# Eight last pairs of a WKV recurrence: every second numerator accumulates in a buffer of the logarithms, and the last pair is finished in two halves

## The chip, the core and the metric

The kernel runs on one core of a Trainium2 chip. The core has five engines with an instruction queue each: TensorE (PE, matrix products into PSUM), VectorE (DVE), ScalarE (ACT, functions such as exponential and logarithm), GpSimd (POOL) and SyncE (SP, which here only issues DMAs). They run beside each other and wait for each other through semaphores. The metric is the time of one execution on the device in microseconds (us), as the median of several executions.

## What is computed

For each of 16 sequences of 2048 steps and each of 256 channels the reference runs a recurrence with a running maximum `pp`, a weighted sum `aa` of the values and a sum `bb` of the weights:

```python
for t in range(seq_len):
    kk, vv = k[b, t, :], v[b, t, :]
    ww = u + kk
    qq = np.maximum(pp, ww)
    e1 = np.exp(pp - qq)
    e2 = np.exp(ww - qq)
    output[b, t, :] = (e1 * aa + e2 * vv) / (e1 * bb + e2 + 1e-08)
    ww = pp - w + kk
    qq = np.maximum(ww, kk)
    e1 = np.exp(ww - qq)
    e2 = np.exp(kk - qq)
    aa = e1 * aa + e2 * vv
    bb = e1 * bb + e2
    pp = qq
```

`k`, `v` and the output are 16 x 2048 x 256 in float32, 33.55 MB each. What matters for this study is the division: every output is a numerator over a denominator.

## The kernel before

**Tiles and stages.** Time is cut into 16 chunks of 128 steps, and the 16 sequences into four groups of four. One such group in one chunk is a "pair" in the kernel's numbering, `n` = 0 to 63, with `c, j = divmod(n, 4)`; a pair's output is a tile of 128 partitions (steps) by 1024 elements, 512 KB. A pair goes through an input part (load, rounding of `k`, logs of weights by TensorE, exponentials by ScalarE at L205, product with the values by VectorE at L214), and four pairs of a chunk together give the chunk's state (`state_*`, a chain of small steps over ScalarE and VectorE that ends in `turn_back`, L297 on TensorE, and `copy_back`, L301 on VectorE). About ten pairs later comes the output part, of which this study speaks:

- `den` (L320): the denominator. Twelve TensorE matmuls (`apply`, L317), three groups of four, into one of the two tiles `X0` and `X1`. The third group of four needs `cb`, the state of the chunk before it is copied back by L301.
- `log_den` (L323): ScalarE takes the logarithm of that tile into a tile `rd` (L325), and gives the `X` tile back.
- `inverse` (L328): ScalarE takes exp(-x) of `rd` in place (L329). So the inverse of the denominator is exp(-ln).
- `num` (L331): the numerator. Twelve matmuls of the same form (L317) into the tile `num`.
- `mult` (L335): VectorE multiplies `num` by `rd` into the output tile `ot` (L337), and gives `num` and `rd` back.
- `store` and `store_rest` (L350, L343): the output tile goes out in three DMAs. SP issues the first half of its columns (256 KB) and one quarter (128 KB); for the pairs from 52 on, GpSimd issues the other quarter (128 KB).

**PSUM and the buffers.** PSUM holds `X0`, `X1` and `num` with two banks each, and one bank each for `TOT` and `TURN`. So there are two buffers for denominators (which the logs of the input part use too, as long as there is input) and one for numerators. `rd` has two buffers, `ot` eight.

**What sets the order.** All instructions of an engine run in the order in which the program emits them. The kernel makes a list of named steps, each with a wished place, the steps that must be emitted before it, and a buffer that it takes and gives back (`step`, and the loop at the end). The loop emits the step with the smallest place whose forerunners are emitted and whose buffer is free in this bookkeeping: `take="X"` needs one of the two `X` tiles, `"N"` the one `num` tile. A step is named here by its kind and pair: LN.59 is the logarithm of pair 59, and so DEN, INV, NUM, MUL, ST (store by SP) and SQ (the quarter by GpSimd).

After the last input pair (63), the output parts of the pairs 55 to 63 are left. In this tail only these steps run, and the last chunk's state chain, which ends in BK.15 (L301); the pairs 60 to 63 need it. TensorE's order there is DEN.56, NUM.55, DEN.57, NUM.56, DEN.58, NUM.57, the turn back of chunk 15, DEN.59, NUM.58, DEN.60, NUM.59 and so on to DEN.63, NUM.62, NUM.63.

Of the kernel before, what the change touches and what calls it, by code (L numbers as in the profile page):

```python
# [7 lines left out]
F32 = mybir.dt.float32  # L8
# [3 lines left out]
ACT = mybir.ActivationFunctionType  # L12
# [3 lines left out]
def kernel(  # L16
# [9 lines left out]
    K = tc.keep_in_program_order  # L26
    PE, DVE, SC, POOL, SP = nc.tensor, nc.vector, nc.scalar, nc.gpsimd, nc.sync
# [5 lines left out]
    D = 2 * Dm  # L33
    NP = 4 * NST
# [5 lines left out]
    BYSP = 3  # L40
    EARLY = 10
    PLAN = "DDDP"
# [1 line left out]
    RS = 2.0 ** -20  # L44
    CAP = 54.0
    BIG = 1e30
    CF = 11
    BYPOOL = 52
    BYQ = "PSSP"
    BYF = 93  # L50
# [7 lines left out]
         "TAIL": {"DEN": -4.36, "LN": -16.54, "INV": 3.8, "NUM": -0.31, "MUL": 4.39, "ST": 14.35, "step": 2.989, "SQ": 26.08},  # L58
         "Z0": {"L": 1, "S": 3, "DEN": 0, "NUM": 6, "TK": 47, "TU": 17, "R": 12},
         "Z": {"DEN": 0, "L": 1, "NUM": 0, "TK": 4, "S": 0, "TU": 1, "R": 0}}  # L60

    consts = ctx.enter_context(tc.tile_pool(name="consts", bufs=1))
    kpool = ctx.enter_context(tc.tile_pool(name="kpool", bufs=NK))
    kppool = ctx.enter_context(tc.tile_pool(name="kppool", bufs=NKP))
    vpool = ctx.enter_context(tc.tile_pool(name="vpool", bufs=NV))
    vbpool = ctx.enter_context(tc.tile_pool(name="vbpool", bufs=NVB))
    rpool = ctx.enter_context(tc.tile_pool(name="rpool", bufs=NRD))
    opool = ctx.enter_context(tc.tile_pool(name="opool", bufs=NOT))
    small = ctx.enter_context(tc.tile_pool(name="small", bufs=2))
    psx = ctx.enter_context(tc.tile_pool(name="psx", bufs=1, space=bass.MemoryType.PSUM))  # L70
    psn = ctx.enter_context(tc.tile_pool(name="psn", bufs=1, space=bass.MemoryType.PSUM))
# [10 lines left out]
    def matrix(name, dt):  # L82
        return consts.tile([128, 128], dt, tag=name, name=name)
# [4 lines left out]
    def rows_of(x, n):  # L88
        c, p = divmod(n, 4)
        return x[4 * p:4 * p + 4, c * TC:(c + 1) * TC, :].rearrange("n t d -> t n d")  # L90

    KR, VR, VB = {}, {}, {}

    def how(n):
        return "D" if n < BYSP else "C" if n < CF else PLAN[n % len(PLAN)]

    def raw(pool, tag):
        return pool.tile([128, 4, Dm], F32, tag=tag, name=tag)

    def load_k(n):  # L100
        if how(n) != "C":
            KR[n] = raw(vpool, "vr") if n < BYSP else raw(kppool, "kf")
            K((SP if n < BYSP else POOL).dma_start(out=KR[n], in_=rows_of(k, n)))  # L103
        else:
            KR[n] = kpool.tile([128, 4, Dm], F32R, tag="kr", name="kr")
            K(POOL.dma_start(out=KR[n], in_=rows_of(k, n)))

    def load_v(n):
        vr = raw(vpool, "vr")
        K((SP if n < BYSP else POOL).dma_start(out=vr, in_=rows_of(v, n)))  # L110
        VR[n] = vr

    WUf = rpool.tile([128, 2, D], F32, tag="rd", name="WUf")[:, 0, 0:Dm]
    WU = consts.tile([128, Dm], BF16, tag="WU", name="WU")

    def row_wu(x, g):
        K(SC.dma_start(out=WUf[g::32, :], in_=bass.AP(tensor=x.tensor, offset=x.offset, ap=[[0, 4], list(x.ap[0])])))

    K(DVE.memset(WUf, 0.0))
    load_k(0)  # L120
    row_wu(w, 0)
    row_wu(u, 1)
    K(SC.preload_act_table_set("natural_log_exp_and_others"))
    M1, I1 = matrix("M1", F32), matrix("I1", F32)
    K(DVE.memset(M1, -1.0))
# [47 lines left out]
    mats = {name: matrix(name, BF16) for name in ("Id", "IdN", "S", "SN")}  # L173
# [11 lines left out]
    X = [psx.tile([128, 2, D], F32, tag=f"X{a}", name=f"X{a}") for a in range(2)]  # L185
# [119 lines left out]
    RD, NUM, OT = {}, {}, {}  # L305
# [17 lines left out]
    def log_den(n, a):  # L323
        rd = rpool.tile([128, 2, D], F32, tag="rd", name="rd")
        K(SC.activation(rd, X[a], ACT.Ln, scale=RS))  # L325
        RD[n] = rd

    def inverse(n):  # L328
        K(SC.activation(RD[n], RD[n], ACT.Exp, scale=-1.0))  # L329

    def num(n):  # L331
        NUM[n] = psn.tile([128, 2, D], F32, tag="num", name="num")
        apply(NUM[n], n, ("SN", "IdN"), 0)

    def mult(n):  # L335
        o = opool.tile([128, 4, Dm], F32, tag="ot", name="ot")
        K(DVE.tensor_mul(o.rearrange("p (i n) d -> p i (n d)", i=2), NUM.pop(n), RD.pop(n)))  # L337
        OT[n] = o

    def piece(n, h, queue):  # L340
# [17 lines left out]
    ops, free = {}, {"K": NK, "KP": NKP, "V": NV, "N": 1, "RD": NRD, "OT": NOT, "VB": NVB}  # L358

    def step(name, place, fn, args=(), after=(), take=None, give=(), mode=0):  # L360
        ops[name] = dict(place=place, fn=fn, args=args, after=list(after), take=take, give=give, mode=mode)

    for n in range(NP):
        c, j = divmod(n, 4)
        early = n < BYSP
        put = lambda key: n + P[key][j]
        lead = SOON * max(0.0, 1 - n / UNTIL)
        m = n + LAG - lead
        tail = n >= NP - LAG
        place = lambda key: m + (P["TAIL"][key] + (n - NP + LAG) * P["TAIL"]["step"] if tail else P["OUT"][key][j])  # L370
        kb = "V" if early else "KP" if how(n) != "C" else "K"
        if n:
            step(("LK", n), n + P["LK"], load_k, (n,), [("LK", n - 1)], kb)
        else:
            free["V"] -= 1
        step(("LV", n), n + P["LV"], load_v, (n,), [("LV", n - 1)] + ([("LK", n)] if n else []), "V")
        if how(n) != "C":
            step(("RK", n), put("RK"), round_k, (n,), [("LK", n), ("RK", n - 1)], "K", [kb])
        for q in range(2):
            step(("R", q, n), n + P["R"][q], rows, (n, q), ["wu", ("R", 1 - q, n - 1 + q)], "X", mode=3)  # L380
            step(("L", q, n), n + P["L"][q], logs, (n, q), [("R", q, n), ("LK", n), ("RK", n), ("L", 1 - q, n - 1 + q)], None,
                 ["K"] if q else [], 1)
            step(("X", q, n), n + P["X"][q], exps, (n, q), [("L", q, n), ("NUM", n - RING), ("S", n - RING)], None, ["X"])
        step(("CV", n), put("CV"), cast_v, (n,), [("LV", n), ("CV", n - 1)], "VB", ["V"])
        step(("TV", n), put("TV"), times_v, (n,), [("X", 1, n), ("CV", n), ("TV", n - 1)], None, ["VB"])
        step(("S", n), put("S"), sums, (n,), [("TV", n), ("S", n - 1)] + ([("CS", c - 1)] if j == 0 else []), mode=2)
        if j == 3:
            s = P["STATE"][0 if c == 0 else 2 if c == NST - 1 else 1]
            for i, (name, fn, *after) in enumerate((
                    ("CS", copy_sums, ("S", n)), ("TU", turn, ("CS", c), ("CH", c - 1)), ("SL", state_logs, ("TU", c)),  # L390
                    ("FR", state_frames, ("SL", c), ("SN", c - 1)), ("OF", state_offsets, ("FR", c)),
                    ("SW", state_weights, ("OF", c)), ("CH", state_chain, ("SW", c), ("KP", c - 1)),
                    ("SS", state_spread, ("CH", c)), ("TK", turn_back, ("SS", c), "mats"), ("BK", copy_back, ("TK", c)),
                    ("SN", state_next, ("OF", c)), ("KP", state_keep, ("CH", c)))):
                if not (name in ("SN", "KP") and c + 1 == NST):
                    step((name, c), n + s[i] - lead * SHARE, fn, (c,), after, mode=1)
        step(("DEN", n), place("DEN"), den, (n,), [("BK", c), ("DEN", n - 1), "mats"], "X", mode=3)
        step(("LN", n), place("LN"), log_den, (n,), [("DEN", n), ("INV", n - 1)], "RD", ["X"])
        step(("INV", n), place("INV"), inverse, (n,), [("LN", n)])
        step(("NUM", n), place("NUM"), num, (n,), [("BK", c), ("TV", n), ("NUM", n - 1), "mats"], "N", mode=3)  # L400
        step(("MUL", n), place("MUL"), mult, (n,), [("NUM", n), ("INV", n), ("MUL", n - 1)], "OT", ["N", "RD"])
        step(("ST", n), place("ST"), store, (n,), [("MUL", n), ("ST", n - 1)], None, [] if shared(n) else ["OT"])
        if shared(n):
            step(("SQ", n), place("SQ"), store_rest, (n,), [("ST", n)], None, ["OT"])
# [4 lines left out]
    xs, held = [0, 1], {}  # L409
    todo = sorted(ops, key=lambda x: ops[x]["place"])  # L410
    while todo:
        for name in todo:
            o = ops[name]
            if all(x not in ops or "done" in ops[x] for x in o["after"]) and (xs if o["take"] == "X" else free.get(o["take"], 1)):
                break
        else:
            raise AssertionError(todo[:9])
        todo.remove(name)
        args = list(o["args"])
        if o["take"] == "X":  # L420
            held[name] = xs.pop(0)
            args.append(held[name])
        elif o["take"]:
            free[o["take"]] -= 1
        elif name[0] == "L":
            args.append(held[("R",) + name[1:]])
        if o["give"] == ["X"]:
            x = held[("DEN", name[1]) if name[0] == "LN" else ("R",) + name[1:]]
            xs.append(x)
            args.append(x)  # L430
        else:
            for x in o["give"]:
                free[x] += 1
        if o["mode"] and not quiet:
            zeros(P["Z0" if name[-1] < FILL else "Z"].get(name[0], 0))
        quiet = quiet and name[0] != "BK" or name[0] == "TK"
        o["fn"](*args)
        o["done"] = True
# [30 lines left out]
```

## Time and profile before

| | |
|---|---|
| median of 3 runs | 294.86 us (294.6 to 296.09) |
| the profiled execution | 294.72 us |
| its span, first to last instruction | 293.0 us |
| mean granted clock of TensorE | 0.987 |
| the last exponential of the input part starts | 258.45 us |
| the last product (L337) | 285.67 to 286.89 us |

The profile is of one execution. Times in it count from the span's start. A row of the timeline has the start, the duration, the engine, the source line, the operation, output<-input with its shape, a count, and in brackets the idle time of the engine before it with what ended it. A row of the groups has the count, busy time and mean, then the idle time. "num" and "X" name the PSUM tiles, so in the kernel before DEN shows as `X<-EZR`, and NUM as `num<-EZR`.

### The profile page before, as it was taken

The page shows a single profiled execution, that of the slowest core. Times are in us where ns is not written, and L with a number is a line of the kernel's source. Part 1 is how long each engine was busy: PE and PEld are TensorE (multiplying, and loading weights), DVE is VectorE, ACT ScalarE, POOL GpSimd, SP SyncE. Part 2 cuts the span into 40 slices and gives each one's busy share as a digit, 9 for nine tenths or more (in the row PEclk, how much of TensorE's full clock was granted, in tenths as well). Part 3 has the DMA queues.
Part 4 walks back from the last instruction along what each step waited for, and adds up shares of the span by engine and source line. Part 5 has one row for each costly group of instructions (what it writes and reads, how often), then busy time and mean ns, then how long its engine had stood idle before and what let it go on. Part 6 is the DMA issues. An engine that isn't in the chain of part 4 may idle for free.

```text
span 293.0 us, 8081 instructions
## 1 busy us (share of the span) xinstructions
PE 273.6 (93%) x3275; PEld 140.2 (48%) x3275; DVE 247.2 (84%) x422; ACT 258.7 (88%) x289; POOL 175.6 (60%) x218
## 2 busy tenths in 40 slices
PE   7899998999999999999999999999999999997750
PEld 7445743454545444444545444554544454543420
DVE  6574859989898989989898989899899989697751
ACT  1486498999999999999999999999999999997970
POOL 6167339575768677575767686775757574431230
PEclk9999999999999999999999999999999999999995
DMA  7999999999999999999999999999999999956884
GB/s 221 349 240 353 346 350 297 380 365 394 380 397 380 380 391 385 391 378 397 383 391 372 392 388 391 395 387 392 391 386 372 394 359 389 313 156 189 221 245 136
DMA packets 58549, 101.20 MB, mean 345 GB/s; under 512 B 5128, under 2 KB 43536, under 8 KB 58512
## 3 DMA queue, kind: packets, MB, share of 16 engines
q0 software_dynamic: 21216, 65.54, 64.8%
q1 hardware_dynamic: 37280, 35.14, 35.7%
q8 instruction: 25, 0.41, 0.6%
q14 instruction: 12, 0.10, 0.1%
q10 hardware_dynamic: 16, 0.01, 0.0%
HBM read 67.12 MB, written 33.55 MB: 344 GB/s over the span
## 4 chain that ended last, share of the span: by engine, by line
PE 70%; DMA 10%; DVE 5%; issue 5%; ACT 4%; POOL 3%; POOLq 0%; SPq 0%; ACTq 0%; DVEq 0%
PE X L202 17%; PE X L317 15%; PE num L317 12%; PE X L196 10%; PE TURN L144 9%; PE TOT L240 6%; DMA kf<-in_k_dram 4%; DMA vr<-in_v_dram 3%; DVE ot L337 2%; DMA WUf<-in_u_dram 2%; PE TOT L253 2%; ACT EZR L205 1%; DVE EZR L214 1%; PE TURN L297 1%; ACT rd L329 1%
## 5 line engine op out<-in xcount | busy, mean ns | idle before, releaser
L205 ACT ACTIVATE EZR<-X 128x1024 bf16<-128x1024 f32 x128 | 126.8, 1014 | 14.9 <-PE X L202 14.9
L209 POOL CAST vb<-vr 128x1024 bf16<-128x1024 f32 x54 | 56.4, 1044 | 71.3 <-DVE EZR L214 67.9
L337 DVE TENSOR_TENSOR ot<-num,rd 128x1024 f32<-128x1024 f32 x64 | 78.1, 1220 | 8.6 <-PE num L317 5.1
L214 DVE TENSOR_TENSOR EZR<-EZR,vb 128x2048 bf16<-128x2048 bf16 x64 | 77.7, 1217 | 0.3
L329 ACT ACTIVATE rd<-rd 128x1024 f32<-128x1024 f32 x64 | 67.8, 1059 | 2.0
L325 ACT ACTIVATE rd<-X 128x1024 f32<-128x1024 f32 x64 | 65.7, 1026 | 3.5 <-PE X L317 1.2
L144 PE MATMUL TURN<-Z 128*128 128x192 bf16 x331 | 56.4, 259 | 1.6 <-DVE Z L128 1.6
L110 POOL DMA_DIRECT2D vr<-in_v_dram x61 | 46.0, 755 | 13.9 <-DVE kr L189 7.1
L196 PE MATMUL X<-WU,CO 64*64 64x512 bf16 x512 | 51.9, 390 | 1.6 <-DVE WU L171 1.3
L144 PEld LDWEIGHTS <-Z 128*128 128x128 bf16 x331 | 29.6, 101 | 48.9 <-issue 47.1
L202 PE MATMUL X<-kr,NLE 128*128 128x512 f32 x128 | 45.6, 438 | 0.0
L202 PE MATMUL X<-kr,NLZ 128*128 128x512 f32 x128 | 45.5, 437 | 0.0
L103 POOL DMA_DIRECT2D kf<-in_k_dram x53 | 40.2, 758 | 0.0
L189 DVE CAST kr<-kf 128x1024 fp32r<-128x1024 f32 x39 | 32.0, 849 | 5.9 <-DMA kf<-in_k_dram 5.8
L317 PE MATMUL num<-EZR,SN 64*64 64x512 bf16 x256 | 25.9, 387 | 6.5 <-DVE ot L337 6.5
L196 PEld LDWEIGHTS <-CO 64*64 64x64 bf16 x512 | 15.7, 105 | 31.8 <-issue 26.9
L317 PE MATMUL X<-EZR,S 64*64 64x512 bf16 x256 | 26.2, 394 | 0.7 <-ACT EZR L205 0.3
L317 PE MATMUL X<-cb,Id 64*64 64x512 bf16 x256 | 25.8, 376 | 0.0
L317 PE MATMUL X<-EZR,Id 64*64 64x512 bf16 x256 | 25.8, 376 | 0.0
L317 PE MATMUL num<-cb,IdN 64*64 64x512 bf16 x256 | 25.8, 378 | 0.0
L317 PE MATMUL num<-EZR,IdN 64*64 64x512 bf16 x256 | 25.6, 376 | 0.0
L240 PE MATMUL TOT<-EZR,OH 128*32 128x256 bf16 x512 | 23.7, 277 | 1.2 <-DVE EZR L214 1.2
(63 smaller groups left out, 259.3 us busy)
## 6 DMA issues: line engine op xcount, KB each, us to landing
vr<-in_v_dram POOLq DMA_DIRECT2D x61, 512.0 KB, 7.8
kf<-in_k_dram POOLq DMA_DIRECT2D x53, 512.0 KB, 8.7
out_dram<-ot SPq DMA_DIRECT2D x64, 256.0 KB, 9.7
out_dram<-ot SPq DMA_DIRECT2D x116, 128.0 KB, 10.0
kr<-in_k_dram POOLq DMA_DIRECT2D x8, 512.0 KB, 8.5
vr<-in_k_dram SPq DMA_DIRECT2D x3, 512.0 KB, 5.2
vr<-in_v_dram SPq DMA_DIRECT2D x3, 512.0 KB, 6.1
out_dram<-ot POOLq DMA_DIRECT2D x12, 128.0 KB, 3.0
```

Source lines behind the costliest of these rows:

```text
L110: K((SP if n < BYSP else POOL).dma_start(out=vr, in_=rows_of(v, n)))
L144: K(PE.matmul(TURN[:, 0:192], Z[:, 0:128], Z, start=first, stop=True, skip_group_check=True))
L196: K(PE.matmul(X[a][o:o + HS, i, :].rearrange("p (n d) -> p n d", n=2), CO[r:r + HS, q, :], WU[r:r + HS, :].unsqueeze(1).broadcast_to([HS, ...
L202: K(PE.matmul(X[a][:, i, :], (NLE, NLZ)[q], km[:, i, :], start=False, stop=True, skip_group_check=True))
L205: K(SC.activation(ez(n)[:, q, 1], X[a], ACT.Exp))
L209: K((DVE if n < EARLY else POOL).tensor_copy(vb, VR.pop(n)))
L214: K(DVE.tensor_mul(ez(n)[:, :, 0], ez(n)[:, :, 1], vb.unsqueeze(1).broadcast_to([128, 2, 2, D])))
L240: K(PE.matmul(t[32 * j:32 * j + 32, 0:256], OH[:, s:s + 32], ez(n)[:, 0, 1 - q, i, 256 * x:256 * x + 256], start=p == 0 and x == 0, stop=p ...
L317: K(PE.matmul(out_tile[o:o + HS, i, :], left, right, start=s == 0, stop=s == 2, tile_position=(r, o), skip_group_check=True))
L325: K(SC.activation(rd, X[a], ACT.Ln, scale=RS))
L329: K(SC.activation(RD[n], RD[n], ACT.Exp, scale=-1.0))
L337: K(DVE.tensor_mul(o.rearrange("p (i n) d -> p i (n d)", i=2), NUM.pop(n), RD.pop(n)))
```

## The change

Two things change in what runs.

- The numerators of the pairs 57, 59, 61 and 63 (`by_x`: the last XT = 8 pairs, odd ones) no longer take the tile `num` but an `X` tile, whichever the bookkeeping has free; the product gives it back. The even pairs keep `num`.
- For the last pair alone (`parts`), the inverse is made in two instructions of 128 x 512, and the product in two instructions of 128 x 512, each half with its own wait. The first half of the output tile is what SP's first store of the pair carries.

The rest of the diff leaves the program as it was at the values given: `FIRST` spells the same choices as before for the pairs 0 to 10, `VOT` is 0, `AT` is empty, and both rows of `row_wu` stay on ScalarE's queue. Up to NUM.56 and DEN.58 every engine has the same instructions in the same order.

```diff
+    XT = 8
...
+    def parts(n):
+        return (slice(0, 1), slice(1, 2)) if n == NP - 1 else (slice(0, 2),)
+
     def inverse(n):
-        K(SC.activation(RD[n], RD[n], ACT.Exp, scale=-1.0))
-
-    def num(n):
-        NUM[n] = psn.tile([128, 2, D], F32, tag="num", name="num")
+        for i in parts(n):
+            K(SC.activation(RD[n][:, i], RD[n][:, i], ACT.Exp, scale=-1.0))
+
+    def by_x(n):
+        return n >= NP - XT and n % 2 == 1
+
+    def num(n, a=None):
+        NUM[n] = psn.tile([128, 2, D], F32, tag="num", name="num") if a is None else X[a]
         apply(NUM[n], n, ("SN", "IdN"), 0)
 
-    def mult(n):
+    def mult(n, a=None):
         o = opool.tile([128, 4, Dm], F32, tag="ot", name="ot")
-        K(DVE.tensor_mul(o.rearrange("p (i n) d -> p i (n d)", i=2), NUM.pop(n), RD.pop(n)))
+        for i in parts(n):
+            K(DVE.tensor_mul(o.rearrange("p (i n) d -> p i (n d)", i=2)[:, i], NUM[n][:, i], RD[n][:, i]))
         OT[n] = o
...
-        step(("NUM", n), place("NUM"), num, (n,), [("BK", c), ("TV", n), ("NUM", n - 1), "mats"], "N", mode=3)
-        step(("MUL", n), place("MUL"), mult, (n,), [("NUM", n), ("INV", n), ("MUL", n - 1)], "OT", ["N", "RD"])
+        step(("NUM", n), place("NUM"), num, (n,), [("BK", c), ("TV", n), ("NUM", n - 1), "mats"], "X" if by_x(n) else "N", mode=3)
+        step(("MUL", n), place("MUL"), mult, (n,), [("NUM", n), ("INV", n), ("MUL", n - 1)], "OT", ["X" if by_x(n) else "N", "RD"])
```

Because `X` tiles are now also held by numerators, the bookkeeping emits TensorE's blocks of the tail in another order. In brackets stands the tile; `num` where none stands before a NUM is the single numerator tile:

```
before: DEN.58[X0] NUM.57[num] TK.15 DEN.59[X1] NUM.58[num] DEN.60[X0] NUM.59[num]
        DEN.61[X1] NUM.60[num] DEN.62[X0] NUM.61[num] DEN.63[X1] NUM.62[num] NUM.63[num]
after:  DEN.58[X0] NUM.57[X1] TK.15 NUM.58[num] DEN.59[X0] DEN.60[X1] NUM.59[X0]
        NUM.60[num] DEN.61[X1] DEN.62[X0] NUM.61[X1] NUM.62[num] DEN.63[X0] NUM.63[X1]
```

The order on ScalarE, VectorE, GpSimd and SP is the one before, but for the split of INV.63 and MUL.63. No DMA is added, removed or moved to another queue.

More of the change, by code (lines that the diff above doesn't have):

```diff
@@ L46 @@
     BIG = 1e30
-    CF = 11
+    FIRST = "DDDCCCCCCCC"
+    VOT = 0
+    XT = 8
     BYPOOL = 52
@@ L60 @@
          "Z": {"DEN": 0, "L": 1, "NUM": 0, "TK": 4, "S": 0, "TU": 1, "R": 0}}
+    AT = {}
     consts = ctx.enter_context(tc.tile_pool(name="consts", bufs=1))
@@ L94, in how @@
     def how(n):
-        return "D" if n < BYSP else "C" if n < CF else PLAN[n % len(PLAN)]
+        return "D" if n < BYSP else FIRST[n] if n < len(FIRST) else PLAN[n % len(PLAN)]
     def raw(pool, tag):
@@ L108, in load_v @@
     def load_v(n):
-        vr = raw(vpool, "vr")
+        vr = raw(opool, "ot") if n < VOT else raw(vpool, "vr")
         K((SP if n < BYSP else POOL).dma_start(out=vr, in_=rows_of(v, n)))
@@ L114, with row_wu @@
     WU = consts.tile([128, Dm], BF16, tag="WU", name="WU")
-    def row_wu(x, g):
-        K(SC.dma_start(out=WUf[g::32, :], in_=bass.AP(tensor=x.tensor, offset=x.offset, ap=[[0, 4], list(x.ap[0])])))
+    def row_wu(queue, x, g):
+        K(queue.dma_start(out=WUf[g::32, :], in_=bass.AP(tensor=x.tensor, offset=x.offset, ap=[[0, 4], list(x.ap[0])])))
     K(DVE.memset(WUf, 0.0))
     load_k(0)
-    row_wu(w, 0)
-    row_wu(u, 1)
+    row_wu(SC, w, 0)
+    row_wu(SC, u, 1)
     K(SC.preload_act_table_set("natural_log_exp_and_others"))
@@ L360, in step @@
     def step(name, place, fn, args=(), after=(), take=None, give=(), mode=0):
-        ops[name] = dict(place=place, fn=fn, args=args, after=list(after), take=take, give=give, mode=mode)
+        key = name if isinstance(name, str) else " ".join(map(str, name))
+        ops[name] = dict(place=AT.get(key, place), fn=fn, args=args, after=list(after), take=take, give=give, mode=mode)
     for n in range(NP):
@@ L365 @@
         early = n < BYSP
+        vb = "OT" if n < VOT else "V"
         put = lambda key: n + P[key][j]
@@ L375 @@
             free["V"] -= 1
-        step(("LV", n), n + P["LV"], load_v, (n,), [("LV", n - 1)] + ([("LK", n)] if n else []), "V")
+        step(("LV", n), n + P["LV"], load_v, (n,), [("LV", n - 1)] + ([("LK", n)] if n else []), vb)
         if how(n) != "C":
@@ L383 @@
             step(("X", q, n), n + P["X"][q], exps, (n, q), [("L", q, n), ("NUM", n - RING), ("S", n - RING)], None, ["X"])
-        step(("CV", n), put("CV"), cast_v, (n,), [("LV", n), ("CV", n - 1)], "VB", ["V"])
+        step(("CV", n), put("CV"), cast_v, (n,), [("LV", n), ("CV", n - 1)], "VB", [vb])
         step(("TV", n), put("TV"), times_v, (n,), [("X", 1, n), ("CV", n), ("TV", n - 1)], None, ["VB"])
@@ L426 @@
             args.append(held[("R",) + name[1:]])
[L427 to L433, printed above, removed]
+        for g in o["give"]:
+            if g == "X":
+                x = held[("DEN", name[1]) if name[0] == "LN" else ("NUM", name[1]) if name[0] == "MUL" else ("R",) + name[1:]]
+                xs.append(x)
+                args.append(x)
+            else:
+                free[g] += 1
         if o["mode"] and not quiet:
```

## The prediction

> **What bounds the kernel now.** The change touches only what is emitted after the input has ended, so I read the tail of the profile and not its averages. First the page, then TensorE's tail in stretches of 3.4 us: start and end, PE busy, PE weight loads, VectorE, ScalarE, GpSimd, granted clock, DMA share, GB/s.
>
> ```profile
> span 293.0 us, 8081 instructions
> ```
>
> ```profile
> 275.00:278.40 3.40, 1.96 (x36) 1.14 (x39) 1.88 (x2) 3.20 (x4) 0.84 (x2) 1.00 0.78 205
> 278.40:281.80 3.40, 2.51 (x44) 1.32 (x37) 1.93 (x2) 3.23 (x4) 0.99 (x2) 1.00 0.85 264
> 281.80:285.20 3.40, 1.45 (x24) 0.67 (x23) 1.74 (x2) 2.58 (x3) 0.97 (x2) 0.99 0.86 234
> 285.20:288.60 3.40, 0.38 (x7) 0.00 (x0) 1.22 (x1) 0.00 (x0) 0.84 (x2) 0.50 0.79 237
> ```
>
> TensorE and VectorE are about half idle, and ScalarE is nearly full (3.20 of 3.40). The longest wait of TensorE in the stretch 262 to 293 us (sum, times, longest):
>
> ```profile
> PE num L317 <- DVE ot L337: 6.1, 8, 1.4
> ```
>
> A numerator waits for the product before it to free the one `num` tile. VectorE's tail, from MUL.56 on (MUL.63 is the last), shows the other side, products that wait for the numerator:
>
> ```profile
> 269.85 1.22 DVE L337 TENSOR_TENSOR ot<-num,rd 128x1024 f32<-128x1024 f32 x1 [1.00 <-DMA out_dram<-ot]
> ...
> 272.21 1.22 DVE L337 TENSOR_TENSOR ot<-num,rd 128x1024 f32<-128x1024 f32 x1
> 273.34 0.69 DVE L301 CAST cb<-TURN 128x512 bf16<-128x512 f32 x1
> 274.43 1.22 DVE L337 TENSOR_TENSOR ot<-num,rd 128x1024 f32<-128x1024 f32 x1 [0.40 <-issue]
> 276.65 1.23 DVE L337 TENSOR_TENSOR ot<-num,rd 128x1024 f32<-128x1024 f32 x1 [1.00 <-PE num L317]
> 278.87 1.22 DVE L337 TENSOR_TENSOR ot<-num,rd 128x1024 f32<-128x1024 f32 x1 [1.00 <-PE num L317]
> ...
> 285.67 1.22 DVE L337 TENSOR_TENSOR ot<-num,rd 128x1024 f32<-128x1024 f32 x1 [1.14 <-PE num L317]
> ```
>
> And TensorE's blocks (first group of four of each), with the turn back ahead:
>
> ```profile
> 272.35 0.40 PE L297 MATMUL TURN<-Id,CB 128*128 128x128 bf16 x4
> 272.68 0.41 PE L317 MATMUL X<-EZR,S 64*64 64x512 bf16 x4
> 272.92 0.39 PE L317 MATMUL X<-EZR,Id 64*64 64x512 bf16 x4
> 273.14 0.39 PE L317 MATMUL X<-cb,Id 64*64 64x512 bf16 x4
> 273.48 0.41 PE L317 MATMUL num<-EZR,SN 64*64 64x512 bf16 x4
> ...
> 277.93 0.41 PE L317 MATMUL num<-EZR,SN 64*64 64x512 bf16 x4 [0.73 <-DVE ot L337]
> ```
>
> MUL.59 starts at 276.65, NUM.60 1.28 later at 277.93, and MUL.60 0.94 after that at 278.87. So 2.22 us a pair are 1.28 + 0.94, a ring of two engines with one buffer. ScalarE (L325 logarithm, L329 inverse; the last two rows are pair 63, those at 273.57 and 275.75 LN.59 and LN.60):
>
> ```profile
> 268.31 1.06 ACT L329 ACTIVATE rd<-rd 128x1024 f32<-128x1024 f32 x1
> 269.27 1.00 ACT L325 ACTIVATE rd<-X 128x1024 f32<-128x1024 f32 x1
> ...
> 273.57 1.02 ACT L325 ACTIVATE rd<-X 128x1024 f32<-128x1024 f32 x1
> ...
> 275.75 1.02 ACT L325 ACTIVATE rd<-X 128x1024 f32<-128x1024 f32 x1
> ...
> 282.41 1.02 ACT L325 ACTIVATE rd<-X 128x1024 f32<-128x1024 f32 x1
> 283.47 1.06 ACT L329 ACTIVATE rd<-rd 128x1024 f32<-128x1024 f32 x1
> ```
>
> An inverse starts 1.06 us after its logarithm (282.41 to 283.47), and the next logarithm can start 0.96 after an inverse (268.31 to 269.27): 2.02 a pair is ScalarE's own pace. It goes at 2.22 because LN.n needs the `rd` tile that MUL.n-2 frees: MUL.58 at 274.43, LN.60 1.32 later at 275.75. So ScalarE's idle time is small, 0.2 a pair, and the ring sets the end. The last pair shows a second loss: INV.63 ends at 284.53, yet MUL.63 starts at 285.67, 1.14 later, for it waits for NUM.63.
>
> **The change part by part.** I take the rows' delays and run them through the new order.
>
> *Start of the chain.* NUM.57 goes into X1 and starts when LN.57 (269.27) has read it, near 270.33, before 271.13. This gains nothing: between MUL.56 and MUL.57 VectorE has the state chain to do, so MUL.57 stays at 272.21, the turn back at 272.35 and BK.15 at 273.34.
>
> *A loss.* TensorE's next block is now NUM.58 and not DEN.59. NUM.58 takes the place at 272.68; with groups at 272.68, 272.92, 273.14, as those rows stand, and 0.22 from group to group, DEN.59 comes at 273.36 instead of 272.68. A block takes 0.43 to its last group and 0.41 more, and ScalarE starts 0.04 after the last end (273.14 + 0.39, then 273.57): 0.88. LN.59 comes at 273.36 + 0.88 = 274.24, 0.67 **later** than before. VectorE meanwhile is early: MUL.58 can start when BK.15 leaves it, at about 273.94, not 274.43.
>
> *The gain in pace.* From LN.59 on, does anything hold ScalarE beyond its 2.02? The `rd` wait: MUL.58 at 273.94 + 1.32 = 275.26, against 276.26 for LN.60. The same holds on, since each product now follows its inverse by 1.09:
>
> ```profile
> 252.33 1.06 ACT L329 ACTIVATE rd<-rd 128x1024 f32<-128x1024 f32 x1
> ```
>
> ```profile
> 253.42 1.23 DVE L337 TENSOR_TENSOR ot<-num,rd 128x1024 f32<-128x1024 f32 x1 [1.34 <-ACT rd L329]
> ```
>
> The new wait is for X: DEN.61 needs X1 from LN.60, and DEN.63 needs X0 from LN.62. A matmul starts 1.06 after the ScalarE instruction that frees its tile:
>
> ```profile
> 258.45 1.01 ACT L205 ACTIVATE EZR<-X 128x1024 bf16<-128x1024 f32 x1
> ```
>
> ```profile
> 259.51 0.41 PE L317 MATMUL X<-EZR,S 64*64 64x512 bf16 x4 [0.33 <-ACT EZR L205]
> ```
>
> So logarithm, denominator, logarithm take 1.06 + 0.88 = 1.94, just under 2.02. Behind the waiting DEN.61 stand DEN.62 and NUM.61; both are needed later than they come. Numerators: NUM.59 waits for LN.59 to leave X0, 275.30, ready for VectorE at 276.24, while INV.59 (275.30) lets MUL.59 start at 276.39; NUM.63 waits for MUL.61 and is ready before INV.63. So LN.63 = 274.24 + 4 x 2.02 = 282.32. That is only 0.09 earlier than 282.41: the late start eats nearly all of the better pace.
>
> *The gap before the last product.* NUM.63 no longer comes last. Uncut, MUL.63 would start at 282.32 + 1.06 + 1.09 = 284.47 and end at 285.69, 1.20 before today's 286.89: 0.09 of it the pace, 1.11 the gap.
>
> *The halves.* No row has an inverse or product of 512; rows of the stretch 255 to 293, grouped by shape, bound them:
>
> ```profile
> L329 ACT ACTIVATE rd<-rd 128x1024 f32<-128x1024 f32 x12 | 12.7, 1056 | 0.3
> ...
> L276 ACT ACTIVATE G<-U 128x192 f32<-128x192 f32 x2 | 0.7, 360 | 0.0
> ```
>
> ```profile
> L337 DVE TENSOR_TENSOR ot<-num,rd 128x1024 f32<-128x1024 f32 x12 | 14.7, 1222 | 6.5 <-PE num L317 5.1 <-DMA out_dram<-ot 1.0 <-issue 0.4
> ...
> L301 DVE CAST cb<-TURN 128x512 bf16<-128x512 f32 x2 | 1.4, 682 | 0.0
> ```
>
> An inverse of 512 lies between 0.36 and 1.06; on the line through both, 0.63. A product of 512 I take as the cast of the same size from PSUM, 0.68 (at least 0.61, half of 1.22; at most 1.22). Instructions that follow each other overlap by about 0.1 on ScalarE and 0.08 on VectorE (272.21 + 1.22 against 273.34, 0.09). First inverse 283.38 to 284.01; first product 284.04; second inverse 283.91 to 284.54; second product 284.64 to 285.32. The halves bring 285.69 - 285.32 = 0.37 (from 0.5 down to a loss of 0.7, were both products as long as a whole one).
>
> *The stores.* Last pair, SP, GpSimd, then each group's median time to landing:
>
> ```profile
> 286.92 0.38 SPq L350 DMA_DIRECT2D out_dram<-ot  x1
> 287.35 0.60 SPq L343 DMA_DIRECT2D out_dram<-ot  x1
> ```
>
> ```profile
> 287.19 0.60 POOL L343 DMA_DIRECT2D out_dram<-ot  x1 [1.75 <-DVE ot L337]
> ```
>
> ```profile
> out_dram<-ot POOLq DMA_DIRECT2D x2, 128.0 KB, 2.9
> out_dram<-ot SPq DMA_DIRECT2D x2, 128.0 KB, 3.0
> ```
>
> Today SP's quarter is the last, 287.35 + 3.0 = 290.35, and the fixed end of the program takes 2.65 more. SP's half needs only the first product and goes near 284.75, so SP's quarter is no longer queued behind it and goes at 285.35; GpSimd's goes 0.30 after the last product, 285.62, landing at 288.52. This is now the last: **290.35 - 288.52 = 1.83 us gained**, 0.09 from ScalarE's pace, 1.11 from the gap, 0.37 from the halves and 0.26 from the stores. Against the profiled execution, 294.72 - 1.83 = 292.89. The median, 294.86, is 0.14 higher, less than the working can tell apart; I say 292.9.
>
> [...] The stretches above show the clock at 1.00 with 1.96 us of TensorE work in 3.4, and at 0.50 after one with 1.45. In the new order a cycle of two pairs (4.04 us) holds two double blocks of 0.65 + 0.84, 2.98 us, which is 2.5 in 3.4, and no pause over 0.6. By these rows the clock holds. [...]
>
> **The rivals.** [...]
>
> 2. *The stores set the end.* The last two products now end 1.65 apart. In the tail landings run from 2.2 to 4.3 us:
>
> ```profile
> DMA to landing us min/median/max: 2.2/3.1/4.3
> ```
>
> At 4.3 for the last quarter 1.4 is lost again: 294.3. Against it: after 285.2 the DMA rate is 237 GB/s, below the 264 of the stretch at 278.4.
>
> 3. *The change doesn't lift the pace.* If a wait that I miss keeps 2.22 a pair, LN.63 comes at 274.24 + 8.88 = 283.12 and 0.80 of the gain is gone: 293.7. For it: the X ring has only 0.08 to spare. Against: exceeding 2.02 by little costs little.
>
> **How the numbers follow.** Forecast 0.66 (292.3 to 293.5), stores 0.14, pace kept 0.11, clock 0.04; 0.05 for what I do not see. About 0.5%, 1.47 us, is what a measurement of this kernel tells from no change. The forecast lies 0.4 beyond it, so about a tenth of its chance falls within: faster 0.62, same 0.33, slower 0.05. The range takes in the forecast's ends, rival 3 and most of rival 2: 292.0 to 294.5.
>
> **What would show it.** Right: LN.59 near 274.2, logarithms 2.0 apart, products straight behind their inverses, NUM.63 not the last to release, the last product near 285.3, the clock at 1.00 until it. Wrong: a DEN.59 that doesn't wait (gain near 2.5), TensorE idle before DEN.61 and DEN.63 with ScalarE waiting, half products well over 0.7, or a last landing over 3.5 us after its issue.

## The result and the profile after

The changed kernel takes 292.66 us (median of 16 executions, 291.82 to 293.5), the kernel before 294.09 us beside it (16 executions, 293.03 to 296.09). The ratio is 0.9949, with a 95% interval from 0.9932 to 0.9966: 1.5 us faster, between 1.0 and 2.0. In a later series the same kernel gave 0.9979 (0.9960 to 0.9998), 0.6 us. Both intervals hold only what lies between 0.9960 and 0.9966, that is 1.0 to 1.2 us, which is the fairest reading. The gain forecast was 1.83.

First the page of the changed kernel, and its tail in stretches of 3.4 us (columns as before: start and end, PE, weight loads, VectorE, ScalarE, GpSimd, clock, DMA share, GB/s).

```profile
span 291.4 us, 8084 instructions
```

```profile
275.20:278.60 3.40, 2.42 (x44) 1.23 (x36) 2.12 (x2) 3.36 (x4) 0.81 (x2) 1.00 0.86 261
278.60:282.00 3.40, 2.85 (x48) 1.54 (x47) 1.84 (x3) 3.35 (x4) 1.21 (x2) 1.00 0.89 241
282.00:285.40 3.40, 0.13 (x4) 0.00 (x0) 2.23 (x3) 1.74 (x3) 1.13 (x2) 1.00 0.98 273
```

ScalarE is now full (3.35 of 3.40) and the clock stays at 1.00 to the last product. The DMA share, 0.98 in the last stretch, comes up again below.

The span is 1.6 us shorter than that of before, but not all of it is the change. MUL.56, which both kernels reach with the same instructions, starts at 269.85 before and at 269.21 here: 0.64 of the 1.6 was there before anything differs. So below, times of the tail are counted from MUL.56. The products (the last row is the two halves of MUL.63, merged):

```profile
269.21 1.22 DVE L349 TENSOR_TENSOR ot<-num,rd 128x1024 f32<-128x1024 f32 x1 [1.00 <-DMA out_dram<-ot]
...
271.56 1.22 DVE L349 TENSOR_TENSOR ot<-X,rd 128x1024 f32<-128x1024 f32 x1
...
273.29 1.21 DVE L349 TENSOR_TENSOR ot<-num,rd 128x1024 f32<-128x1024 f32 x1
275.71 1.23 DVE L349 TENSOR_TENSOR ot<-X,rd 128x1024 f32<-128x1024 f32 x1 [1.21 <-ACT rd L337]
277.71 1.22 DVE L349 TENSOR_TENSOR ot<-num,rd 128x1024 f32<-128x1024 f32 x1 [0.78 <-ACT rd L337]
...
283.29 1.29 DVE L349 TENSOR_TENSOR ot<-X,rd 128x512 f32<-128x512 f32 x2 [0.35 <-ACT rd L337]
```

The products wait no longer for the numerator (`<-PE num`) but for the inverse (`<-ACT rd`). The last one ends at 283.29 + 1.29 = 284.58, 15.37 after MUL.56; before it was 286.89 - 269.85 = 17.04. So the arithmetic ends 1.67 earlier. From there to the span's end it was 293.0 - 286.89 = 6.11, and is now 291.4 - 284.58 = 6.82. Of the 1.67, 0.71 is given back after the last product.

ScalarE from INV.58 to LN.60, and pair 63:

```profile
271.78 1.06 ACT L337 ACTIVATE rd<-rd 128x1024 f32<-128x1024 f32 x1
273.56 1.02 ACT L329 ACTIVATE rd<-X 128x1024 f32<-128x1024 f32 x1 [0.72 <-PE X L321]
274.62 1.06 ACT L337 ACTIVATE rd<-rd 128x1024 f32<-128x1024 f32 x1
275.58 1.01 ACT L329 ACTIVATE rd<-X 128x1024 f32<-128x1024 f32 x1
...
281.59 1.01 ACT L329 ACTIVATE rd<-X 128x1024 f32<-128x1024 f32 x1
282.62 1.15 ACT L337 ACTIVATE rd<-rd 128x512 f32<-128x512 f32 x2
```

LN.59 waits 0.72 us for its denominator, as NUM.58 now stands ahead of it on TensorE:

```profile
272.02 0.41 PE L321 MATMUL num<-EZR,SN 64*64 64x512 bf16 x4
...
272.69 0.39 PE L321 MATMUL X<-EZR,S 64*64 64x512 bf16 x4
```

After it the logarithms come 2.01 apart (273.56, then 281.59 four pairs later), at ScalarE's own pace. The halves, by shape:

```profile
L337 ACT ACTIVATE rd<-rd 128x512 f32<-128x512 f32 x2 | 1.1, 622 | 0.0
```

```profile
L349 DVE TENSOR_TENSOR ot<-X,rd 128x512 f32<-128x512 f32 x2 | 1.3, 686 | 0.3 <-ACT rd L337 0.3
```

What remains are the stores. The last pair's issues by SP and GpSimd, and the time from issue to landing of its two quarters:

```profile
284.08 0.54 SPq L362 DMA_DIRECT2D out_dram<-ot  x1
284.72 1.01 SPq L355 DMA_DIRECT2D out_dram<-ot  x1
```

```profile
284.87 0.60 POOL L355 DMA_DIRECT2D out_dram<-ot  x1 [1.03 <-DVE ot L349]
```

```profile
out_dram<-ot SPq DMA_DIRECT2D x1, 128.0 KB, 4.4
out_dram<-ot POOLq DMA_DIRECT2D x1, 128.0 KB, 3.9
```

They are issued as early as forecast, and land late: 4.4 and 3.9 us against the 3.0 and 2.9 of before.

### The profile page after: what moved, and what is told of

Its sections match the earlier page's. It is cut to its first block, busy times and chain, and to the rows that moved or that the text cites. A ratio compares the mean times of both kernels' runs of the same rounds, so it can differ in the third digit from the quotient of the medians.

```text
span 291.4 us, 8084 instructions
## 1 busy us (share of the span) xinstructions
PE 273.7 (94%) x3275; PEld 140.6 (48%) x3275; DVE 247.1 (85%) x423; ACT 258.4 (89%) x290; POOL 175.7 (60%) x218
## 4 chain that ended last, share of the span: by engine, by line
PE 71%; DMA 7%; DVE 5%; issue 5%; POOL 5%; ACT 4%; POOLq 0%; SPq 0%; ACTq 0%; DVEq 0%
PE X L206 17%; PE X L321 15%; PE num L321 12%; PE X L200 10%; PE TURN L148 9%; PE TOT L244 6%; DMA kf<-in_k_dram 4%; POOL vr L114 2%; DMA WUf<-in_u_dram 2%; PE TOT L257 2%; DVE ot L349 2%; POOL kr L110 2%; ACT EZR L209 1%; ACT rd L329 1%; DVE EZR L218 1%
## 5 line engine op out<-in xcount | busy, mean ns | idle before, releaser
L349 DVE TENSOR_TENSOR ot<-num,rd 128x1024 f32<-128x1024 f32 x60 | 73.2, 1221 | 4.5 <-ACT rd L337 3.2
L337 ACT ACTIVATE rd<-rd 128x1024 f32<-128x1024 f32 (+1 forms) x65 | 67.9, 1046 | 2.0
L148 PE MATMUL TURN<-Z 128*128 128x192 bf16 x331 | 57.0, 262 | 1.6 <-DVE Z L132 1.6
L321 PE MATMUL num<-EZR,SN 64*64 64x512 bf16 x240 | 24.3, 386 | 1.5 <-DVE ot L349 1.5
L321 PE MATMUL num<-cb,IdN 64*64 64x512 bf16 x240 | 24.0, 376 | 0.0
L321 PE MATMUL num<-EZR,IdN 64*64 64x512 bf16 x240 | 23.9, 376 | 0.0
```

Source lines behind the costliest of these rows:

```text
L148: K(PE.matmul(TURN[:, 0:192], Z[:, 0:128], Z, start=first, stop=True, skip_group_check=True))
L321: K(PE.matmul(out_tile[o:o + HS, i, :], left, right, start=s == 0, stop=s == 2, tile_position=(r, o), skip_group_check=True))
L337: K(SC.activation(RD[n][:, i], RD[n][:, i], ACT.Exp, scale=-1.0))
L349: K(DVE.tensor_mul(o.rearrange("p (i n) d -> p i (n d)", i=2)[:, i], NUM[n][:, i], RD[n][:, i]))
```

## The experiments

Theory A: the stores hold the end. With the pairs 2.0 us apart the DMA engines are full, and the last landing follows from the bytes still to go. Rival B: the store tail follows the last product at a fixed distance, and the longer tail of one profile is chance. After the second series a third theory, C, was needed. The table holds all runs: the ratio to before with its interval, and from the profile the end of the last product after MUL.56 and the distance from there to the span's end, in us.

| run | ratio to before | last product | to the end |
|---|---|---|---|
| before | 1 | 17.04 | 6.11 |
| changed kernel | 0.9949 (0.9932 to 0.9966) | 15.37 | 6.82 |
| changed_again | 0.9979 (0.9960 to 0.9998) | 15.37 | 6.87 |
| x_whole | 0.9958 (0.9937 to 0.9978) | 15.74 | 6.20 |
| halves_alone | 0.9990 (0.9967 to 1.0013) | 16.97 | 6.10 |
| x_last | 0.9985 (0.9965 to 1.0005) | 15.87 | 6.79 |
| den_first | 0.9949 (0.9928 to 0.9971) | 14.73 | 7.39 |
| den_whole | 0.9947 (0.9930 to 0.9965) | 15.10 | 6.55 |
| no_62 | 0.9920 (0.9893 to 0.9947) | 15.36 | 5.85 |
| last_by_act | 0.9922 (0.9899 to 0.9945) | 15.36 | 5.73 |
| hw_quarters | 0.9910 (0.9890 to 0.9929) | 15.36 | 4.99 |
| before_hw | 0.9946 (0.9927 to 0.9964) | 17.00 | 4.39 |
| den_hw | 0.9903 (0.9878 to 0.9927) | 14.74 | 5.35 |
| den_whole_hw | 0.9901 (0.9874 to 0.9927) | 15.10 | 4.67 |

**First series: the parts.** x_whole, the X tiles without the halves:

```diff
-        return (slice(0, 1), slice(1, 2)) if n == NP - 1 else (slice(0, 2),)
+        return (slice(0, 2),)
```

> The last pair's inverse and product are whole again, the numerators stay as in the changed kernel. Counted from the start of MUL.56, the last product ended at 17.04 us before and at 15.37 in the changed kernel. Both theories: it ends 0.37 later than in the changed kernel, near 15.75. Theory A (the stores hold the end: with pairs 2.0 us apart the DMA engines of the last 4 us are full, so the last landing follows from the bytes still to go and not from the last product): the span's end stays within 0.2 of the changed kernel, near 22.2 after MUL.56. Theory B (the store tail follows the last product at a fixed distance, and the longer tail of the one profile was chance): the end is 0.4 to 0.6 later than in the changed kernel, and the time with it.

The last product is later by 0.37 as both said, and the distance shrinks from 6.82 to 6.20: by the profile the span ends 0.25 earlier after MUL.56 than with the halves (21.94 for 22.19), and the time can't be told from that of the changed kernel. That speaks against B, which had the end 0.4 to 0.6 later. It is not quite A either, which allowed 0.2. In the stretch that corresponds to the one with a DMA share of 0.98, and for the stores issued after 282, the rows without the halves are:

```profile
281.55:284.95 3.40, 0.14 (x4) 0.00 (x0) 2.17 (x2) 1.66 (x2) 0.77 (x2) 1.00 0.96 271
```

```profile
out_dram<-ot POOLq DMA_DIRECT2D x2, 128.0 KB, 3.0
...
out_dram<-ot SPq DMA_DIRECT2D x2, 128.0 KB, 3.1
```

The DMA engines are nearly as busy, 0.96, and yet the quarters land in 3.0 and 3.1 us, about as before, and the distance is about that of before, 6.11. So pairs 2.0 us apart do not lengthen the tail by themselves. What differs is the last pair: with the halves GpSimd's quarter of pair 63 is issued 1.64 us after that of pair 62 (283.23, 284.87), without them 2.00.

halves_alone, the halves without the X tiles:

```diff
-    XT = 8
+    XT = 0
```

> No numerator goes to an X tile (TensorE in the order of before); only the last pair's inverse and product are cut. Both theories: the last product still waits for NUM.63, so its second half ends near 17.1 after MUL.56, no earlier than before; SP's half goes out 0.5 earlier. The time lies 0 to 0.4 below before. A gain of 1 us or more would speak against both, for then the halves and not the X tiles would carry the change.

As expected: the last product ends at 16.97, and the time is 0.3 us below before, with an interval from 1.0 less to 0.4 more. A gain of 0.37 could hide in it.

x_last, only the last numerator in an X tile, with the halves:

```diff
-    XT = 8
+    XT = 2
```

> Only NUM.63 goes to an X tile, with the halves; pairs 57, 59 and 61 keep the single numerator tile, so the ring keeps 2.22 us a pair until MUL.62, and DEN.59 isn't late. Both theories: LN.63 as before, the last product ends near 15.5 after MUL.56, within 0.2 of the changed kernel, for the pace was worth 0.1. Theory A (stores hold the end): pair 62's stores go out as late as before, the last two pairs' 1 MB needs about 4 us from then, so the end comes within 0.5 of before. Theory B (the end follows the last product): the time is 1.3 to 1.8 below before, as in the changed kernel or better.

A's 4 us for the last 1 MB are an estimate; they agree with the 264 GB/s that the profile of before shows from 278.4 to 281.8. This run tells the theories apart. The arithmetic ends 1.17 before that of before, and the time gains 0.4 us at the middle of an interval that includes nothing and ends at 1.0 (0.9965 to 1.0005). B, with 1.3 to 1.8, or with 1.17 for the product as it came, falls. By the profile the span ends 0.49 earlier after MUL.56 than before, within A's 0.5. GpSimd's quarter of pair 63 is issued only 1.20 us after that of pair 62 here, and both quarters land in 3.8 us, though the pairs ahead of it are 2.2 apart. The product came 0.37 later than I expected, since VectorE still had MUL.62 to finish: the two halves follow it without a pause.

den_first, the late LN.59 mended (79.8 is a place just behind that of DEN.59):

```diff
-    AT = {}
+    AT = {"NUM 58": 79.8}
```

> The changed kernel with NUM.58 emitted behind DEN.59 instead of ahead of it, which takes away the 0.67 us by which LN.59 came late. Both theories: LN.59 waits for its denominator no longer, every later logarithm comes 0.6 to 0.7 earlier, and the last product ends near 14.7 after MUL.56. Theory A (stores hold the end): 0.2 to 0.6 of it reach the time, against the changed kernel. Theory B (the end follows the last product): 0.6 to 0.7 do.

The arithmetic ended where it was expected, 0.64 earlier, and the distance grew by 0.57. The time (0.9949) can't be told from that of the changed kernel (0.9949 and 0.9979). By the profile the span ends 0.07 earlier after MUL.56 than in the changed kernel, less than the 0.2 to 0.6 that A expected. So the loss that the prediction found in the new order was real, but mending it alone brings next to nothing by the profile (the times are too coarse to exclude a few tenths): pair 63's quarters now land in 4.5 and 4.7 us.

**Second series: what in the stores.** changed_again is the changed kernel beside the others, without an edit.

> The changed kernel itself on this chip, so that the next three have it beside them. Theory A (the stores hold the end): again about 6.8 us from the end of the last product to the span's end, not the 6.1 of before. Theory B (that tail was chance): nearer 6.1, and a time lower by the 0.6.

6.87 again: the longer tail is not chance. no_62:

```diff
     def store(n):
+        if n == NP - 2:
+            return
...
     def store_rest(n):
-        piece(n, 1, POOL)
+        if n != NP - 2:
+            piece(n, 1, POOL)
```

> The changed kernel without the three stores of pair 62, so 512 KB of the output is not written. Theory A (the last pair's stores queue behind those of the pair before): the distance from the last product to the span's end falls from 6.8 to 6.1 or less, and the time is 0.6 to 1.2 below the changed kernel. Theory B (a fixed distance): nothing moves by more than 0.2.

With the pair ahead of it gone, the last pair lands sooner and the distance is 5.85. In time it is 0.0029 and 0.0059 below the two series of the changed kernel, 0.9 and 1.7 us. Its landings (GpSimd's quarter 2.8 us, for 3.9 in the changed kernel):

```profile
out_dram<-ot SPq DMA_DIRECT2D x1, 256.0 KB, 2.1
...
out_dram<-ot POOLq DMA_DIRECT2D x1, 128.0 KB, 2.8
```

So the stores of pair 62 hold up those of the last pair: GpSimd's quarter lands 1.1 us sooner (2.8 for 3.9) once they are missing from both queues. By what mechanism, no run shows.

den_whole, the mended order without the halves, is den_first and x_whole in one:

> NUM.58 behind DEN.59, and the last pair's inverse and product whole: the pace without the halves. Theory A: the last product ends near 15.1 after MUL.56, the pairs still come 2.0 us apart, so the stores end as in the run with whole halves or up to 0.6 earlier; the time lies 0 to 0.6 below the changed kernel and level with the cut version of the same order. Theory B: it loses the 0.37 of the halves against that version.

Level with den_first (0.9947 and 0.9949), as A said: again the halves don't show in the time, and by the profile the span ends 0.47 earlier after MUL.56 without them (21.65 for 22.12). The quarters of pair 63 land in 3.4 and 3.5 us, more than in x_whole, though its pairs are 2.0 apart at the end too; here pair 59 came only 1.44 after pair 58 (GpSimd's issues at 275.97 and 277.41), and at 2.0 us a pair that lead may not have been worked off. That last step is argued, not shown.

hw_quarters moves GpSimd's quarter of the last four pairs to hardware queues. The reason was what a MB costs on each queue, in the stretch 275 to 283 of before (q1 is SP's queue, q0 GpSimd's; packets, MB, share of the 16 engines):

```profile
q1 hardware_dynamic: 1422, 1.34, 49.9%
q0 software_dynamic: 190, 0.52, 32.8%
```

```diff
     def shared(n):
-        return n >= BYPOOL or BYQ[n % len(BYQ)] == "P" and n >= BYF
+        return n == NP - 1 or BYPOOL <= n < NP - 4 or BYQ[n % len(BYQ)] == "P" and n >= BYF
...
-        piece(n, 1, POOL)
+        piece(n, 1, SC if n == NP - 1 else POOL)
```

> The changed kernel, with GpSimd's quarter of the pairs 60 to 62 issued by SP and that of pair 63 by ScalarE, which has nothing left to do. In the stretch 275 to 283 of before GpSimd's 0.52 MB took 32.8 per cent of the DMA engines' time and SP's 1.34 MB took 49.9: 63 against 37 per cent for a MB. Theory A: with the quarters at SP's price a pair needs about a sixth less of the engines' time, the tail is full no longer, the distance from the last product to the end falls from 6.8 to 6.0 to 6.4, and the time is 0.3 to 0.8 below the changed kernel. Theory B: the distance doesn't change, or grows by the longer row of SP's issues.

The kernel gains far more than that: the distance falls to 4.99, 1.83 less than in the changed kernel, where A had allowed 0.4 to 0.8, and the time is 1.1 and 2.0 us below the two series of the changed kernel. So A was not the whole. The drains at the program's end show the rest. In these rows of the closing line stand the count, the durations in ns (least, median, most), and the starts of the first and the last; the longest DRAIN of GpSimd is its first. Before, then the changed kernel, then hw_quarters, each with GpSimd and then SP:

```profile
L464 POOLq DRAIN  x3: 46/93/4542, 287.2 to 292.5; - x3
```

```profile
L464 SPq DRAIN  x3: 7/7/7, 290.7 to 292.3; - x3
```

```profile
L478 POOLq DRAIN  x3: 46/93/5482, 284.8 to 291.1; - x3
```

```profile
L478 SPq DRAIN  x3: 7/7/7, 289.4 to 290.9; - x3
```

```profile
L478 POOLq DRAIN  x3: 46/93/4564, 276.9 to 289.1; - x3
```

```profile
L478 SPq DRAIN  x3: 7/7/7, 288.5 to 288.8; - x3
```

SP's first DRAIN stands behind its waits for landings, so its start shows when they are over. Before, GpSimd's drain runs from 287.2 to 291.7, while SP's waits are over at 290.7; read so, the program waits 1.0 us for GpSimd alone. In the changed kernel it is 284.9 + 5.48 = 290.4 against 289.4, 1.0 again. In hw_quarters GpSimd's last store was long ago, its drain is over at 281.5, and the span ends 0.8 after SP's first drain (289.3 against 288.5), not 2.0 to 2.3 as in the other two. Theory C: the end waits for GpSimd's drain, which outlasts SP's waits by 1 us, and whose packets are served late when the pair before is still going out (in no_62, without that pair, it takes 4.38 us for the 5.48 of the changed kernel). The last packet of GpSimd's queue runs at 289.70 to 289.75 before and at 288.35 to 288.40 in the changed kernel; the drain is over 2.0 and 1.9 us later.

**Third series: theory C.** before_hw is the kernel before with the edit of hw_quarters.

> The kernel before (one numerator tile, whole last pair) with the same hardware quarters as in the run above: pairs 60 to 62 by SP, pair 63 by ScalarE. New theory C: the end waits for GpSimd's queue drain, which ends 2.0 us behind the last packet of GpSimd's own stores (before: last SP wait over at 290.8, drain over at 291.8; changed kernel: 289.4 and 290.3), and these packets are served late when the pair before is still going out. Without GpSimd's stores the distance from the last product to the span's end is 5.0, as in the run above, the end near 22.0 after MUL.56, the time 0.9 to 1.3 below before; and the change, on this footing, is worth its 1.67, 1.4 to 1.9 in time. Theory A (only the price of the packets counts): before is not as full, 82.7 per cent, so it gains 0.0 to 0.4.

The price theory alone falls: with the arithmetic unchanged (17.00) the distance drops from 6.11 to 4.39 and the time by 1.6 us (1.1 to 2.1). That is somewhat more than C's 0.9 to 1.3. SP's waits are over 0.5 earlier after MUL.56, too (20.4 for 20.9), which is in keeping with cheaper packets that add to the missing drain. Beside it hw_quarters, of another series, lies at 0.9910 / 0.9946 = 0.9964, 1.1 us, and by the profiles its span ends 21.39 - 20.35 = 1.04 earlier after MUL.56, where the arithmetic gains 1.64. I had expected 1.4 to 1.9: even without GpSimd's drain 0.6 is given back. Of this, 0.37 is the issue: in hw_quarters SP is still issuing the two quarters of pair 62 until 284.37, and its last store goes out 0.81 after the last product (285.12), in before_hw 0.44 (287.25).

last_by_act has only the second half of that edit: pair 63's quarter goes by ScalarE, those of 60 to 62 stay with GpSimd.

```diff
-        piece(n, 1, POOL)
+        piece(n, 1, SC if n == NP - 1 else POOL)
```

> The changed kernel, and only the quarter of pair 63 goes by ScalarE; GpSimd keeps those of 60 to 62. Theory C: GpSimd's last packets are now pair 62's, its drain ends before SP's waits do, and the time is 0.9 to 1.6 below the changed kernel, nearly as good as with all four quarters moved. Theory A (price of the packets): three of the four dear quarters stay, so at most 0.4 is gained.

C is borne out: 0.9922 against 0.9949 and 0.9979 for the changed kernel, 0.8 and 1.7 us less, though three of the four dear quarters stay. By the profile the span ends 1.10 earlier after MUL.56 (21.09 for 22.19). It is not nearly as good as hw_quarters, which ends at 20.35: the other three quarters are worth another 0.7 by the profiles, which is in keeping with a price that counts too. GpSimd's longest drain now ends before SP is through (283.7 + 4.86 = 288.6 against 289.6):

```profile
L478 POOLq DRAIN  x3: 46/249/4857, 283.7 to 290.6; - x3
```

```profile
L478 SPq DRAIN  x3: 7/7/7, 289.6 to 289.9; - x3
```

den_hw and den_whole_hw put all together, the latter without the halves; their edits stand above.

> All together: the changed kernel, NUM.58 behind DEN.59, hardware quarters. Last product near 14.7 after MUL.56. Theory C: the distance to the end is 5.0 to 5.6 (the stores' own bytes begin to hold it), the time 0.1 to 0.6 below the run with hardware quarters alone. Theory A: the same, or no gain at all because the engines are full.

> The same as the run before it, but the last pair's inverse and product whole. If the halves are worth nothing because the stores hold the end, the time is within 0.2 of it; if they were worth nothing only because of GpSimd's drain, it is 0.3 to 0.5 higher.

Both have the lowest times of all: 290.93 us and 290.77 us beside 293.74 of before, 2.8 and 3.0 us faster. They can't be told apart; by the profile den_whole_hw ends 0.32 earlier after MUL.56, though its last product is 0.36 later. But this pair is no fair test of the halves, for SP's issues hold them up. In den_hw, from the quarters of pair 62 on:

```profile
282.55 1.25 SPq L355 DMA_DIRECT2D out_dram<-ot  x2
283.89 0.54 SPq L362 DMA_DIRECT2D out_dram<-ot  x1
284.53 0.59 SPq L355 DMA_DIRECT2D out_dram<-ot  x1
```

The first half product ends at 282.85, but SP is busy with pair 62 until 283.80. Its first store of pair 63 leaves 15.18 after MUL.56, in den_whole_hw 15.13, and its last store 15.82 and 15.55. So the halves bring no earlier store there at all, and the last one goes out 0.27 later. What the halves would be worth without GpSimd's drain and with a free queue was not tried; whether den_hw beats hw_quarters (0.9903 and 0.9910) stays open as well.

## Why the prediction held, and the step that failed

**The start of the chain, and the loss at LN.59:** right. From MUL.56, LN.59 was forecast at 274.24 - 269.85 = 4.39 and came at 273.56 - 269.21 = 4.35. den_first shows it from the other side: with the order mended the arithmetic ends 0.64 earlier.

**The pace:** right, 2.01 for 2.02 us a pair, with inverse and product 1.09 apart (274.62 to 275.71). The X ring did not hold it.

**The gap and the halves:** right in the arithmetic. Last product at 15.37, forecast 285.32 - 269.85 = 15.47; a half inverse 0.622 for 0.63, a half product 0.686 for 0.68. But the 0.37 of the halves counts as a gain only if the stores follow, and in three pairs of runs (changed kernel and x_whole, den_first and den_whole, den_hw and den_whole_hw) they don't: the times, good to about 0.6 us, show no gain, and by the profiles the span ends later with the halves, by 0.25, 0.47 and 0.32. Without the halves the forecast was 1.20, and x_whole gave 1.30 in the arithmetic, 23.15 - 21.94 = 1.21 in the span counted from MUL.56, and 1.2 us in time (0.6 to 1.9).

**The stores:** this step failed. It read "landing at 288.52. This is now the last", with landings as long as before and a "fixed end of the program", and it gave a gain of 0.26. By it the span would have ended 5.85 after the last product. Measured were 6.82 and 6.87, so the term was wrong by 1.0 and has the other sign: -0.71. Two things stood in its place. First, what ended last was GpSimd's drain, already before the change, and not SP's quarter. It begins with GpSimd's last issue, 0.30 after the last product before and 0.29 with the change, so an earlier issue by SP could not bring the end forward. Its row was in the profile of before (4542 ns from 287.2), and I didn't read it. Second, the landing time was no constant. With the halves the last pair's stores follow those of pair 62 more closely; its quarters took 3.9 and 4.4 us, and the drain 5.48 instead of 4.54, 0.94 more. From the drain to the span's end it is 1.3 before and 1.1 with the change, which gives 0.2 back; the profiles show no reason for that. Where the quarters land in 2.9 to 3.1 us, before and in x_whole, the drain takes 4.54 and 4.63 and the distance is 6.11 and 6.20. The prediction had named the sign itself: a last landing over 3.5 us after its issue. With 1.67 in place of 1.57 for the arithmetic and -0.71 in place of 0.26, the sum is 0.96 instead of 1.83; the two timed series say 1.5 and 0.6.

**The time:** 292.66 for a forecast of 292.9 is nearer than the working deserves, and partly luck. The forecast took 1.83 off the profiled 294.72, while the kernel before came to 294.09 beside the changed one, 0.63 lower. That more than made up for the 0.4 by which the gain fell short in that series; in the later one it fell short by about 1.

**The rivals:** the 0.04 for a fall of the clock was an estimate, and no run shows such a fall in the new order: TensorE waits 0.48 to 0.51 us for ScalarE four times, at 274.64 to 280.64, and the granted clock stands at 1.00 in every stretch from 265.0 to 285.4. Rival 2, the stores, was the larger part of what happened: I had priced it at 1.4 and given it 0.14, for the DMA rate at the end, 237 GB/s, lay below the 264 of the stretch from 278.4. The rate was the wrong row. The share of busy DMA engines would not have been enough either, since x_whole has 0.96 and lands as before. The prediction had the number that mattered, the last two products 1.65 apart, and didn't ask what it does to the landings. Rival 3 is out, the pace did rise.

## What to carry to other kernels

Here arithmetic that ended 1.67 us earlier brought 1.0 to 1.2 us in time, and 0.71 was given back after the last product. At the end of a program, then, work out how closely the last stores will be issued behind each other and whether their queue is free, and read the drains of each engine that issues stores, before taking the distance from the last result to the end as fixed. Where one queue's drain outlasts the others, let another queue issue the last store; here moving one 128 KB store of the last pair was worth 0.8 and 1.7 us (last_by_act), about as much as the whole change to the last eight with 1.5 and 0.6. And compare two profiles from the first instruction that differs, since two executions of the same instructions here were 0.64 us apart ahead of it.

## What the runs showed of the hardware

- GpSimd's closing drain begins with the issue of its last store and takes 4.34 us (before_hw) to 6.08 us (den_first) in these runs. Where both engines store the last pair, SP's waits for landings are over 0.9 to 1.1 us before it.
- Stores by GpSimd's software queue took 63% of the DMA engines' time for a MB in that stretch of 8 us, stores by SP's hardware queue 37% (before, 275 to 283: 32.8% for 0.52 MB and 49.9% for 1.34 MB). That is not the shape of the quarters alone: in hw_quarters, where SP issues more of them, its queue took 70.5% for 1.81 MB in the same stretch, 39% for a MB.
- A share of busy DMA engines near 1 did not tell how late a store lands: the last quarters landed in 3.0 and 3.1 us at a share of 0.96 where GpSimd issued its last quarter 2.00 us after the one ahead (x_whole), in 3.9 and 4.4 us at 0.98 where it was 1.64 (changed kernel).
- An earlier issue ended later here: with the halves SP's first store of the last pair went out 0.9 us earlier (14.87 after MUL.56 for 15.76) and the span ended 0.25 later (22.19 and, in changed_again, 22.24 for 21.94).
